# Host-laid parameters, memory and S5 array, S5's short kernels ahead of its scan, and gate blocks and branch work spread differently, in a one-core hybrid trunk

## The chip, the cores and the metric

One core of one Trainium2 chip runs the whole kernel. The metric is the device time of one execution in microseconds (us). TensorE is written PE, its weight loads PEld, VectorE DVE, ScalarE ACT, GpSimd POOL and SyncE SP; SP issues most of the DMA loads, POOL most of the stores.

## What is computed

One decoder layer on 1024 tokens of width 1024, all in float32, then a final norm:

```
h = rms_norm(x, norm_mix)
p_rw, p_s5, p_gla, p_gate = split(h @ w_in)
merged = sum_i sigmoid(p_gate_i) * (mixer_i @ w_branch_i)   # i: RWKV-7, S5, GLA
x += merged @ w_out
x += cross_attention(rms_norm(x), rms_norm(mem), ...)        # keys, values: mem_n @ xa_wkv
x += conv_ffn(rms_norm(x), ...)
```

S5 has 32 groups of 16 channels, each a complex diagonal recurrence of 64 states, `s_t = abar * s_(t-1) + B u_t`, `y = gelu(Re(C s) + d u)`, followed by `y * sigmoid(y @ w_glu + b_glu)`. RWKV-7 carries a 64 x 64 state for each of 8 heads through the 1024 tokens. The gates are 24 blocks of 128 columns of `w_in` (3 mixers x 8 blocks).

## The kernel before

A float32 product of full accuracy is three matmuls: both operands are split into a high and a low part in a rounded format (`split`, L145: ACT writes `whi`, DVE subtracts and writes `wlo`), and `mm3` (L161, the matmuls are L163 to L165) adds high x high, high x low and low x high. Weights come in units of 256 KB (`wunit`, L150: a DMA on SP's queue into `wraw`, then the split). `fm_block` (L172) makes 128 output columns for all 1024 tokens: 8 k-tiles x 2 halves x 3 = 48 matmuls of 512 columns into `ps_fm`. A gate block (`gate_block`, L1057) is one `fm_block`, a sigmoid on ACT and a store. Other matmuls (transposes, S5's and RWKV's products) are plain float32 with 128 columns.

The stages follow each other in program order. A scheduler orders each engine's instructions by priority, and a later, independent piece of work fills in where an earlier one waits; on each engine the order is then fixed.

- **start** (L258): the two memory tiles are loaded, transposed on PE, split into `mT`; the rows of small parameters (`vectors`, L86) come in by one DMA each and are turned to columns by a transpose on PE (`ps_v`). `kv_k` makes the keys (8 blocks of 24 matmuls of 256 columns; the eviction to `ko` multiplies by the memory's norm `mrb`), `x` is loaded, normed and transposed into `hT`, `kv_v` makes the values.
- **s5** (L357, `s5_states` L384): the parameters are loaded and transposed, powers of `abar` are computed on DVE. Then, for each of two halves of the groups: two `fm_block`s make `U` (via a DRAM array); per quad of groups `ps_ht` (transposes, copied by ACT to `ht`) and `ps_in` make the scan's input; DVE runs the scan (13 steps of 4 operations on `s5s`); ACT copies the states (L553, four copies); per quad a product on DVE makes `GA` (L558), PE the short kernel `ps_k` (L563), which goes to DRAM and comes back as `s5m` by eight loads (L573); ACT copies `GA` to `s5g` (L577); PE makes `ps_y` from both (L585, L586), ACT the gelu (L588), PE the transposes `ps_yt`. The `filler` of 11 gate blocks stands behind all this in the program. Then `s5h` is split and the GLU's 96 matmuls run.
- **gla**, then **rw_setup** and **rw1** with three gate blocks between its parts and ten behind it (`gates[14:]`).
- **rw2** (L909): 16 groups of four chunks. `rw2_prods` makes six products in a row, `vl`, `w1`, `x1`, `z`, `qm` among them, each copied out by ACT or DVE before it is an operand; `z` needs `w1`, `qm` needs `z`. `rw2_steps` carries the state: three matmuls for each chunk, then DVE and ACT each write half of the next state, on which the next chunk's third matmul waits. `fill` (in `run`) hands out the branch products of S5 and GLA in 16 pieces behind `step`.
- **conv_consts** (L122) loads and transposes the FFN's convolution weights late, before the attention.

Of the kernel before, what the change touches and what calls it, by code (L numbers as in the profile page):

```python
# [40 lines left out]
class Trunk:  # L41
# [44 lines left out]
    def vectors(self, p):  # L86


        nc, cp, A = self.nc, self.cp, self.A
        rows = [("nmem", A["norm_mem"], 8), ("nmix", A["norm_mix"], 8), ("mu", A["rw_mu"], 14), ("w0", A["rw_w0"], 4),  # L90
                ("a0", A["rw_a0"], 4), ("kk", A["rw_k_k"], 4), ("ka", A["rw_k_a"], 4), ("rk", A["rw_r_k"], 4),
                ("lnw", A["rw_ln_w"], 4), ("lnb", A["rw_ln_b"], 4), ("bglu", A["s5_b_glu"], 4),
                ("nxa", A["norm_xattn"], 8), ("nffn", A["norm_ffn"], 8), ("gkb", A["gla_gk_b"], 2), ("gnorm", A["gla_norm"], 1)]
        nrow = sum(n for _, _, n in rows)
        self.vc = cp.tile([128, nrow], F32, name="vc")
        self.cv = cp.tile([128, 176], F32, name="cv")
        self.omu = cp.tile([128, 14], F32, name="omu")
        self.omka = cp.tile([128, 4], F32, name="omka")
        self.vo = {}
        vr = [p.tile([n, 128], F32, name=f"vr{n}") for n in (16, nrow - 16)]  # L100

        def load(part, t, r0):
            for name, ap, n in part:
                o = self.vo[name] = sum(x[2] for x in rows[:[x[0] for x in rows].index(name)])
                flat = ap if len(ap.shape) == 1 else ap.rearrange("a b -> (a b)") if len(ap.shape) == 2 \
                    else ap.rearrange("a b c -> (a b c)")
                nc.sync.dma_start(t[o - r0:o - r0 + n, :], flat.rearrange("(n p) -> n p", p=128))

        def columns(t, r, n):
# [10 lines left out]
        load(rows[:2], vr[0], 0)  # L120
        columns(vr[0], 0, 16)
        return others  # L122

    def conv_consts(self):
        nc, A = self.nc, self.A
        with ExitStack() as c2:
            p = self.pool(c2, "crows")
            for i in range(2):
                r0, n = (0, 128) if i == 0 else (128, 48)
                vr = p.tile([128, 128], F32, name=f"cr{i}")  # L130
                if i == 0:
                    nc.sync.dma_start(vr[:, :], A["ffn_conv"].rearrange("a b c -> (a b c)").rearrange("(n p) -> n p", p=128)[0:128])
                else:
                    nc.sync.dma_start(vr[0:4, :], A["ffn_conv"].rearrange("a b c -> (a b c)").rearrange("(n p) -> n p", p=128)[128:132])
                    nc.sync.dma_start(vr[4:48, :], A["ffn_conv_b"].rearrange("a b -> (a b)").rearrange("(n p) -> n p", p=128))
                ps = self.psm.tile([128, 512], F32, tag="m", name="ps_cv")
                nc.tensor.transpose(ps[:, :n], vr[:n, :], self.ident[:n, :n])
                nc.vector.tensor_copy(self.cv[:, r0:r0 + n], ps[:, :n])
# [122 lines left out]
    def start(self, pool):  # L261

        self.hT = self.new_T(pool, "hT")
        with ExitStack() as c2:
# [17 lines left out]
            mem = [load(self.A["mem"][0, tt * 128:tt * 128 + 128, :]) for tt in range(2)]  # L282
            other_vectors = self.vectors(p)

            self.mT = {(k, l): p.tile([128, 256], F32R, name=f"mT{k}{l}") for k in range(8) for l in range(2)}
            self.to_fm(mem, "nmem", lambda k, l: self.mT[k, l][:])
            self.mrs = scales(mem)
            ones = p.tile([128, 128], F32, name="ones")
            self.nc.gpsimd.memset(ones[:], 1.0)
            self.mrb = p.tile([128, 256], F32, name="mrb")  # L290
            dg = p.tile([128, 256], F32, name="dg")
            for i in range(2):
                self.nc.vector.tensor_scalar(dg[:, i * 128:i * 128 + 128], self.ident[:], self.mrs[:, i:i + 1], None, op0=ALU.mult)
            ps = self.psm.tile([128, 512], F32, tag="m", name="ps_rb")
            self.nc.tensor.matmul(ps[:, :256], ones[:], dg[:], start=True, stop=True)
            self.nc.scalar.copy(self.mrb[:], ps[:, :256])
# [8 lines left out]
            self.kv_k(0)  # L305
            self.kv_k(1)
            load_x()
# [3 lines left out]
            norm_half(0)  # L311
            self.kv_v(0)
            norm_half(1)
            for j in range(1, 4):
                self.kv_v(j)
# [41 lines left out]
    def s5(self, filler):  # L357
# [4 lines left out]
        with ExitStack() as c1:  # L362
            po = self.pool(c1, "s5o")
            YT = [po.tile([128, T], F32, name=f"s5yt{b}") for b in range(4)]
            with ExitStack() as c2:
                p = self.pool(c2, "s5p")
                self.s5_states(p, YT, KD, UD)
                filler()
# [15 lines left out]
    def s5_states(self, p, YT, KD, UD):  # L384
# [3 lines left out]
        rows = p.tile([48, 128], F32, tag="kp", name="s5rows")  # L388
        ls = p.tile([48, 2], F32, name="s5ls")
        nc.sync.dma_start(rows[0:16, :], A["s5_a_re"][0].rearrange("(g r) n -> g (r n)", r=2))  # L390
        nc.sync.dma_start(rows[16:32, :], A["s5_a_im"][0].rearrange("(g r) n -> g (r n)", r=2))
        nc.sync.dma_start(ls[32:48, :], A["s5_log_step"][0].rearrange("(g r) -> g r", r=2))
        v.tensor_copy(rows[32:48, :].rearrange("p (r n) -> p r n", r=2), ls[32:48, :].unsqueeze(2).to_broadcast([16, 2, 64]))
        ps = self.psm.tile([128, 512], F32, tag="m", name="ps_s5")
        nc.tensor.transpose(ps[:, :48], rows[:, :], ident[:48, :48])
        par = p.tile([128, 48], F32, name="s5par")
        v.tensor_copy(par[:], ps[:, :48])
        ar, ai, lst = par[:, 0:16], par[:, 16:32], par[:, 32:48]
        B = [p.tile([128, 16, 16], F32, name=f"s5b{i}") for i in range(2)]
        C = [p.tile([128, 16, 16], F32, name=f"s5c{i}") for i in range(2)]  # L400
        for i, (bn, cn) in enumerate((("s5_b_re", "s5_c_re"), ("s5_b_im", "s5_c_im"))):
            nc.sync.dma_start(B[i][:], A[bn][0].rearrange("g n c -> (g n) c").rearrange("(g q) c -> q g c", q=128))
            cr = p.tile([128, 4, 64], F32, tag=f"hs{i}", name=f"s5cr{i}")
            nc.sync.dma_start(cr[:], A[cn][0].rearrange("g c n -> (g c) n").rearrange("(t q) n -> q t n", q=128))
            ps = self.psm.tile([128, 512], F32, tag="m", name="ps_c")
            for t in range(4):
                nc.tensor.transpose(ps[0:64, t * 128:t * 128 + 128], cr[:, t, :], ident[:])
            pv = ps[0:64, :].rearrange("p (g r c) -> p g r c", r=2, c=16)
            for r in range(2):
                v.tensor_copy(C[i][r * 64:r * 64 + 64], pv[:, :, r, :])  # L410
        dcol = p.tile([128, 4], F32, name="s5d")
        dr = p.tile([4, 128], F32, name="s5dr")
        nc.sync.dma_start(dr[:], A["s5_d"][0].rearrange("g c -> (g c)").rearrange("(t q) -> t q", q=128))
        ps = self.psm.tile([128, 512], F32, tag="m", name="ps_d")
        nc.tensor.transpose(ps[:, :4], dr[:], ident[:4, :4])
        v.tensor_copy(dcol[:], ps[:, :4])
# [70 lines left out]
        for hf in range(2):  # L487


            for b in range(2):  # L490
# [7 lines left out]
                for t in range(8):  # L498
                    nc.sync.dma_start(U[t * 16:t * 16 + 16, b * 8:b * 8 + 8, :], UD[c0:c0 + 128, t, :].rearrange("(g c) j -> c g j", c=16))
            for qd in range(2):  # L500
# [14 lines left out]
                for jj in range(2):  # L515
                    ps = self.psm.tile([128, 512], F32, tag="m", name="ps_in")
                    for j2 in range(2):
                        j = jj * 2 + j2
                        for i in range(2):
                            for r in range(2):  # L520
# [5 lines left out]
                                  ps[:].rearrange("p (g i j) -> p g i j", g=2, i=2))  # L526

# [381 lines left out]
    def rw2(self, p, p0, fill):  # L909
# [21 lines left out]
        n = 0  # L931
        todo, prev = [], []

        def step():
            pr, g, ops = todo.pop(0)
            with self.tc.high_priority(200):
                prev.append((pr, g, self.rw2_steps(p, pr, g, ops, S0)))
# [729 lines left out]
```

## Time and profile before

| | |
|---|---|
| median of 3 runs | 2225.42 us (2224.3 to 2226.51) |
| the profiled execution | 2228.63 us, its span 2226.9 us |
| mean granted PE clock | 0.988 |
| busy: PE, DVE, ACT, POOL | 2123.9, 1447.8, 961.0, 196.3 us |
| matmuls | 10,704 |

The span runs from the first to the last instruction on the profile; 1.7 us of the execution lie around it. PE's busy time is 95% of the span, so about 103 us of the span are its idle time. The clock of 1.00 is 2.4 GHz; the only other level is half of it. The busy shares are means over stages which differ; the rows below are from single stages.

### The profile page before, as it was taken

The page shows a single profiled execution, that of the slowest core. Times are in us where ns is not written, and L with a number is a line of the kernel's source. Part 1 is how long each engine was busy: PE and PEld are TensorE (multiplying, and loading weights), DVE is VectorE, ACT ScalarE, POOL GpSimd, SP SyncE. Part 2 cuts the span into 40 slices and gives each one's busy share as a digit, 9 for nine tenths or more (in the row PEclk, how much of TensorE's full clock was granted, in tenths as well). Part 3 has the DMA queues.
Part 4 walks back from the last instruction along what each step waited for, and adds up shares of the span by engine and source line. Part 5 has one row for each costly group of instructions (what it writes and reads, how often), then busy time and mean ns, then how long its engine had stood idle before and what let it go on. Part 6 is the DMA issues. An engine that isn't in the chain of part 4 may idle for free.

```text
span 2226.9 us, 29866 instructions
## 1 busy us (share of the span) xinstructions
PE 2123.9 (95%) x10704; PEld 1738.8 (78%) x10704; DVE 1447.8 (65%) x2870; ACT 961.0 (43%) x1667; POOL 196.3 (9%) x292
## 2 busy tenths in 40 slices
PE   7999989999999999999999999999899999988997
PEld 7878779888888888888788787877677777766886
DVE  7783733554667761667686656657777777777756
ACT  6324243553554431333343544446444444453452
POOL 1000000001211221002200000000011111110000
PEclk9999999999999999999999999999999999999999
DMA  7423331112334465665564232332565566588332
GB/s 246 137 88 95 94 97 54 29 52 67 134 112 128 135 186 152 171 157 141 136 214 148 87 104 72 89 119 81 137 157 159 139 150 128 123 241 286 104 96 102
DMA packets 318878, 286.65 MB, mean 129 GB/s; under 512 B 92532, under 2 KB 253129, under 8 KB 318729
## 3 DMA queue, kind: packets, MB, share of 16 engines
q1 hardware_dynamic: 291385, 207.64, 32.7%
q0 software_dynamic: 27344, 77.08, 12.7%
q8 instruction: 85, 1.39, 0.3%
q14 instruction: 64, 0.52, 0.1%
HBM read 190.32 MB, written 94.34 MB: 128 GB/s over the span
## 4 chain that ended last, share of the span: by engine, by line
PE 78%; DVE 10%; ACT 4%; DMA 4%; issue 2%; SPq 1%; DVEq 0%; ACTq 0%
PE ps_fm L163 10%; PE ps_fm L165 10%; PE ps_fm L164 10%; PE ps_q L1287 5%; PE ps_q L1288 5%; PE ps_q L1289 5%; PE ps_dm L1461 4%; PE ps_dn L1461 4%; PE ps_tm L163 3%; PE ps_tm L165 3%; PE ps_tm L164 3%; DVE wlo L148 2%; PE ps_g L868 1%; ACT whi L147 1%; DMA araw<-d_act 1%
## 5 line engine op out<-in xcount | busy, mean ns | idle before, releaser
L148 DVE TENSOR_TENSOR wlo<-wraw,whi 128x512 fp32r<-128x512 f32 (+1 forms) x318 | 219.7, 692 | 278.4 <-ACT whi L147 276.1
L147 ACT CAST whi<-wraw 128x512 fp32r<-128x512 f32 (+1 forms) x318 | 196.5, 619 | 472.0 <-PE ps_fm L164 283.0
L163 PE MATMUL ps_fm<-hT,whi 128*128 128x512 f32 x800 | 319.1, 399 | 0.0
L164 PE MATMUL ps_fm<-hT,whi 128*128 128x512 f32 x800 | 317.5, 397 | 0.0
L165 PE MATMUL ps_fm<-hT,wlo 128*128 128x512 f32 x800 | 317.4, 397 | 0.0
L163 PEld LDWEIGHTS ps_fm<-hT,whi 128*128 128x128 f32 x800 | 151.8, 190 | 33.1 <-issue 1.2
L165 PEld LDWEIGHTS ps_fm<-hT,wlo 128*128 128x128 f32 x800 | 151.5, 189 | 33.1 <-issue 0.6
L164 PEld LDWEIGHTS ps_fm<-hT,whi 128*128 128x128 f32 x800 | 151.8, 190 | 32.6 <-issue 0.8
L1287 PE MATMUL ps_q<-a,whi 128*128 128x512 f32 x336 | 134.9, 402 | 13.1 <-ACT u L1362 5.6
L1289 PE MATMUL ps_q<-a,wlo 128*128 128x512 f32 x336 | 134.1, 399 | 1.1 <-DVE wlo L148 1.1
L1288 PE MATMUL ps_q<-a,whi 128*128 128x512 f32 x336 | 134.0, 399 | 0.0
L1300 DVE SCALAR_TENSOR_TENSOR c<-u,cvn,c 128x1023 f32<-128x1023 f32 x84 | 107.7, 1283 | 22.2 <-ACT c L1298 20.8
L1309 POOL DMA_DIRECT2D d_act<-c x77 | 65.9, 862 | 438.5 <-DVE c L1304 320.5
L165 PE MATMUL ps_tm<-whi,a 128*128 128x512 f32 x256 | 101.3, 396 | 0.0
L1461 PE MATMUL ps_dn<-whi,b 128*128 128x512 f32 x312 | 98.6, 393 | 2.8 <-ACT whi L147 2.8
L147 ACT CAST whi<-s 128x512 fp32r<-128x512 f32 x84 | 52.1, 620 | 105.3 <-PE ps_q L1288 80.9
L147 ACT CAST b<-araw 128x512 fp32r<-128x512 f32 x72 | 44.7, 620 | 101.3 <-PE ps_dn L1461 37.6
L1287 PEld LDWEIGHTS ps_q<-a,whi 128*128 128x128 f32 x336 | 64.4, 192 | 29.5 <-ACT u L1362 6.9
L1461 PE MATMUL ps_dm<-whi,b 128*128 128x512 f32 x264 | 84.0, 398 | 2.4 <-ACT whi L147 2.4
L148 DVE TENSOR_TENSOR wlo<-s,whi 128x512 fp32r<-128x512 f32 x84 | 57.6, 688 | 36.3 <-ACT whi L147 35.3
L163 PE MATMUL ps_fm<-a,whi 128*128 128x512 f32 x192 | 78.7, 410 | 2.3 <-ACT whi L147 2.2
L148 DVE TENSOR_TENSOR b<-araw,b 128x512 fp32r<-128x512 f32 x72 | 49.6, 690 | 47.1 <-ACT b L147 46.9
(551 smaller groups left out, 5058.9 us busy)
## 6 DMA issues: line engine op xcount, KB each, us to landing
wraw<-in_w_in SPq DMA_DIRECT2D x104, 256.0 KB
araw<-d_act SPq DMA_DIRECT2D x77, 256.0 KB
d_act<-c POOLq DMA_DIRECT2D x22, 768.0 KB, 7.6
d_gate<-gate SPq DMA_DIRECT2D x24, 512.0 KB
gsg<-d_gate SPq DMA_DIRECT2D x24, 512.0 KB
wraw<-in_ffn_w_up SPq DMA_DIRECT2D x46, 256.0 KB
d_act<-c POOLq DMA_DIRECT2D x11, 1024.0 KB, 6.1
d_act<-c POOLq DMA_DIRECT2D x44, 256.0 KB, 5.1
```

The source lines that it names most:

```text
L147: self.nc.scalar.copy(hi, src)
L148: self.nc.vector.tensor_tensor(lo, src, hi.bitcast(F32), op=ALU.subtract)
L163: nc.tensor.matmul(ps, lh, rh, start=first, stop=False)
L164: nc.tensor.matmul(ps, lh, rl, start=False, stop=False)
L165: nc.tensor.matmul(ps, ll, rh, start=False, stop=last)
L868: nc.tensor.matmul(ps[:, j * 128:j * 128 + 128], BD[i][:, ci, :], AR[:, :, ci * 64:ci * 64 + 64], start=True, stop=True)
L1287: nc.tensor.matmul(ps, hi[:, s], t[0][:], start=first and k == 0, stop=False, skip_group_check=True)
L1288: nc.tensor.matmul(ps, hi[:, s], t[1][:], start=False, stop=False, skip_group_check=True)
L1289: nc.tensor.matmul(ps, lo[:, s], t[0][:], start=False, stop=last and k == 3, skip_group_check=True)
L1300: v.scalar_tensor_tensor(c[:, d:], src[:, :T - d], cw(2 - d), c[:, d:], op0=ALU.mult, op1=ALU.add)
L1309: to = lambda n0, n1, h, **kw: nc.gpsimd.dma_start(st(n0, n1), src[h].to_broadcast([128, n1 - n0, 512]), **kw)
L1461: nc.tensor.matmul(o, a[x][:, s], w[y], start=first and k == 0, stop=last and k == 2, skip_group_check=True)
```

## The change

The host lays out five things instead of the kernel: all small parameter columns (`cols`, one load to `vc`), the convolution columns (`conv`, one load to `cv`; `conv_consts` is gone), the S5 parameters as one array of 128 x 1076 values (`s5pk`, 551 KB, the first load on SP's queue), and the memory transposed (`memT`). The memory in its own layout is still loaded, for its norm, behind all of `x`; keys leave PE without the norm and are multiplied by `mrb` later, eight in a row.

```diff
+            for u in range(4):
+                self.nc.sync.dma_start(raw[u][:], self.A["memT"][u * 256:u * 256 + 256, :].rearrange("(k p) t -> p k t", p=128))
+                if u < 2:
+                    us.append(self.wunit(self.A["xa_wkv"][0][u * 512:u * 512 + 512, :128], 4, 128))
...
+            self.kv_k(0, us)
+            load_x()
+            self.kv_k(1)
+            self.kv_k(2)
+            self.kv_k(3)
+            load_x()
+            norm_half(0)
+
+            self.mrs = scales([load(self.A["mem"][0, tt * 128:tt * 128 + 128, :]) for tt in range(2)])
+            self.kv_v(0)
+            norm_half(1)
...
+            for j, o in enumerate(self.keys):
+                self.nc.vector.tensor_tensor(o[:], o[:], mrb[:], op=ALU.mult)
+                self.nc.gpsimd.dma_start(self.d_k[j * 128:j * 128 + 128, :], o[:])
```

In S5 the per-quad product `GA`, the short kernel `ps_k`, its way through DRAM and the loads of `s5m` (now two buffers) move ahead of the scan as `kernels(qd)`; the copies to `s5g` become `gains`, the first quad's ahead of the scan, the second's behind it. The gate blocks are handed out one place at a time: two behind `U`, three ahead of the scan, one behind it, for each half, and one before the GLU, 13 in all.

```diff
+            fill(2)
             for qd in range(2):
...
+            GA, M0 = kernels(0)
+            G0 = gains(GA)
+            GA, M1 = kernels(1)
+            fill(3)
...
                     nc.scalar.copy(S2[i * 64:i * 64 + 64, :, r, :], S[r * 64:r * 64 + 64, i, :, 0:128])
+            fill(1)
             for qd in range(2):
...
+                G, M = (gains(GA), M1) if qd else (G0, M0)
...
-                    self.gate_block(*gates[11 + pr])
+                    self.gate_block(*gates[13 + pr])
...
-            for g in gates[14:]:
+            for g in gates[16:]:
```

In rw2 the branch products are cut into 32 pieces (26 and 6, where there were 13 and 3) and handed out between `x1` and `z` and behind `qm`; the step of the group before stands between `z` and `qm`.

```diff
-                    todo.append((pr, hf * 2 + g2, self.rw2_prods(p, g2 * 4, t, R, c3)))
-                    if len(todo) > 1:
+                    z, qm = self.rw2_prods(p, g2 * 4, t, R, c3)
+                    fill()
+                    z()
+                    if todo:
                         step()
+                    todo.append((pr, hf * 2 + g2, qm()))
+                    norm()
+                    fill()
```

What the scheduler makes of it, at three places. First SP's queue at the program's beginning; `wraw<-in_xa_wkv` are the units of the key weights, two for each block of keys. Before:

```order
L269 DMA xt<-in_mem 128x1024 x2
L107 DMA vr_134<-in_norm_mem 8x128
L107 DMA vr_134<-in_norm_mix 8x128
L156 DMA wraw<-in_xa_wkv 128x4x128 x4
L269 DMA xt<-in_x 128x1024
L156 DMA wraw<-in_xa_wkv 128x4x128 x4
L269 DMA xt<-in_x 128x1024 x3
L156 DMA wraw<-in_xa_wkv 128x4x128
L269 DMA xt<-in_x 128x1024
```

And now:

```order
L1527 DMA s5pk<-in_s_par 128x1076
L95 DMA vc<-in_cols 128x81
L253 DMA memT_131<-in_memT 128x2x256
L122 DMA wraw<-in_xa_wkv 128x4x128
L253 DMA memT_132<-in_memT 128x2x256
L122 DMA wraw<-in_xa_wkv 128x4x128
L253 DMA memT_133<-in_memT 128x2x256
L253 DMA memT_134<-in_memT 128x2x256
L122 DMA wraw<-in_xa_wkv 128x4x128 x2
L235 DMA xt<-in_x 128x1024 x4
L122 DMA wraw<-in_xa_wkv 128x4x128 x4
L235 DMA xt<-in_x 128x1024
```

The memory's two tiles came first and the third key block's units stood behind one tile of `x`; now the S5 array, the columns and the first part of the memory come first, the memory's other parts among the first four units, and the third block's units stand behind four tiles of `x`.

Second, ACT's queue behind S5's first scan: `s5s` is the copy of the states (L553 before, L540 now), `s5g` the copy of `GA` (L577, L506), `s5yg` the gelu (L588, L553), `gate` the sigmoid of a gate block. Before:

```order
L553 COPY s5s_1652<-s5s 64x8x128 x4
L577 COPY s5g<-ga_1657 64x4x128 x2
L577 COPY s5g<-ga_1658 64x4x128 x2
L147 CAST whi<-wraw 128x512 x2
L1061 ACTIVATE gate<-ps_fm 128x1024
L147 CAST whi<-wraw 128x512 x2
L1061 ACTIVATE gate<-ps_fm 128x1024
L588 ACT_TABLE_LOAD
L588 ACTIVATE s5yg<-ps_y 128x4x8x16 x2
L577 COPY s5g<-ga_1718 64x4x128
```

And now, from the last sigmoid during the scan on:

```order
L1041 ACTIVATE gate<-ps_fm 128x1024
L540 COPY s5s_1985<-s5s 64x8x128 x4
L113 CAST whi<-wraw 128x512 x2
L1041 ACTIVATE gate<-ps_fm 128x1024
L113 CAST whi<-wraw 128x512
L553 ACT_TABLE_LOAD
L553 ACTIVATE s5yg<-ps_y 128x4x8x16 x2
L506 COPY s5g<-ga_1679 64x4x128
```

Of the first quad's copies to `s5g`, which stood between the copy of the states and the weight splits, nothing is left there; the second quad's still stand behind the first quad's gelu, which waits for PE.

Third, PE's queue in rw2 around one group. `ps_z` and `ps_qm` are the dependent products, `ps_p` with `s_` the state's matmul, `ps_fm` the branch work. Before:

```order
L979 MATMUL ps_w_8183<-R_8155,wx_7947 128x128 x4
L979 MATMUL ps_x_8190<-wv_7942,wak_7936 128x128 x4
L979 MATMUL ps_z<-qw_8188,qvl 128x128 x4
L163 MATMUL ps_fm<-a_7869,whi 128x512
L164 MATMUL ps_fm<-a_7870,whi 128x512
L165 MATMUL ps_fm<-a_7869,wlo 128x512
L163 MATMUL ps_fm<-a_7875,whi 128x512
L979 MATMUL ps_qm<-qz,wa_7939 128x128
L1013 MATMUL ps_p<-qx_8043,qz 128x128
L1014 MATMUL ps_p<-wv_7926,R_7969 128x128
L1016 MATMUL ps_p<-s_0_0_7952,qqm 128x128
```

And now:

```order
L951 MATMUL ps_z<-qw_8162,qvl 128x128
L993 MATMUL ps_p<-qx_8054,qz 128x128
L994 MATMUL ps_p<-wv_7863,R_7906 128x128
L996 MATMUL ps_p<-s_0_0_7889,qqm 128x128
L951 MATMUL ps_z<-qw_8162,qvl 128x128 x3
L129 MATMUL ps_fm<-a_7806,whi 128x512
L130 MATMUL ps_fm<-a_7807,whi 128x512
L131 MATMUL ps_fm<-a_7806,wlo 128x512
L993 MATMUL ps_p<-qx_8054,qz 128x128
L994 MATMUL ps_p<-wv_7863,R_7906 128x128
L996 MATMUL ps_p<-s_0_1_7891,qqm 128x128
L951 MATMUL ps_qm<-qz,wa_7876 128x128 x4
```

The three or four `ps_fm` matmuls between `ps_z` and `ps_qm` are still there, with a step of the chain among them; what is new is a run of 24 `ps_fm` matmuls right ahead of the first row, between `ps_x` and `ps_z`. In the whole of rw2 the runs of `ps_fm` number 77 before and 48 now.

## Rows read from the trace of the kernel before

**Rows 1.** the page's header, its engine row and its chain row.

```profile
span 2226.9 us, 29866 instructions
...
PE 2123.9 (95%) x10704; PEld 1738.8 (78%) x10704; DVE 1447.8 (65%) x2870; ACT 961.0 (43%) x1667; POOL 196.3 (9%) x292
...
PE 78%; DVE 10%; ACT 4%; DMA 4%; issue 2%; SPq 1%; DVEq 0%; ACTq 0%
```

**Rows 2.** windows: stretch, us, busy time and count per engine, PEclk, DMA share, GB/s.

```profile
0.00:20.00 20.00, 10.90 (x67) 10.01 (x67) 10.54 (x40) 12.28 (x23) 1.73 (x11) 1.00 0.89 274
20.00:40.00 20.00, 16.36 (x132) 15.71 (x131) 13.43 (x34) 12.86 (x25) 3.45 (x6) 1.00 0.83 267
74.13:330.22 256.09, 235.38 (x1213) 190.58 (x1212) 154.28 (x367) 85.10 (x121) 5.81 (x11) 0.96 0.33 97
884.33:1149.70 265.37, 252.84 (x1581) 213.80 (x1580) 192.12 (x460) 95.28 (x192) 28.20 (x30) 0.99 0.61 164
```

**Rows 3.** waits of PE in the S5 stage, 74 to 331 us: total, times, longest.

```profile
PE ps_k L563 <- DVE ga L332: 9.9, 2, 5.1
PE ps_ht L513 <- DVE hs L332: 2.6, 1, 2.6
PE ps_y L586 <- DMA s5m<-s_k: 2.5, 1, 2.5
PE ps_y L585 <- ACT s5g L577: 1.9, 1, 1.9
PE ps_fm L163 <- ACT s5h L147: 1.8, 1, 1.8
```

**Rows 4.** waits of PE in the start, 0 to 75 us.

```profile
PE ps_fm L163 <- DVE ko L1114: 2.6, 3, 1.8
```

**Rows 5.** PE's timeline: start, duration, engine, line, operation, [idle before].

```profile
74.13 0.48 PE L163 MATMUL ps_fm<-hT,whi 128*128 128x512 f32 x1
...
149.65 0.39 PE L164 MATMUL ps_fm<-hT,whi 128*128 128x512 f32 x1
...
158.84 0.39 PE L165 MATMUL ps_fm<-hT,wlo 128*128 128x512 f32 x1
164.29 0.40 PE L563 MATMUL ps_k<-ga,s5bd 128*32 128x128 f32 x2 [5.06 <-DVE ga L332]
```

**Rows 6.** DVE's timeline, S5's first scan: first operation, last, and the product's end.

```profile
129.52 1.23 DVE L538 TENSOR_TENSOR sc<-s5s,s5l 128x1024 f32<-128x1024 f32 x1
...
160.81 1.20 DVE L541 TENSOR_TENSOR s5s<-s5s,sc 128x1008 f32<-128x1008 f32 x1
...
166.43 0.46 DVE L559 TENSOR_SCALAR ga<-ga 128x576 f32<-128x576 f32 x1
```

**Rows 7.** ACT's timeline, behind S5's two scans.

```profile
162.05 4.21 ACT L553 COPY s5s<-s5s 64x1024 f32<-64x1024 f32 x4 [5.91 <-DVE s5s L541]
166.27 2.53 ACT L577 COPY s5g<-ga 64x512 f32<-64x512 f32 x4
...
288.96 1.28 ACT L588 ACT_TABLE_LOAD   x1
290.26 1.08 ACT L588 ACTIVATE s5yg<-ps_y 128x512 f32<-128x512 f32 x2
```

**Rows 8.** SP's queue in S5, 169 to 176 us.

```profile
169.81 0.34 SPq L570 DMA_DIRECT2D s_k<-kp  x1
...
172.37 3.82 SPq L573 DMA_DIRECT2D s5m<-s_k  x8
```

**Rows 9.** waits of PE in rw2, 884 to 1150 us.

```profile
PE ps_qm L979 <- DVE qz L997: 6.1, 6, 2.3
PE ps_fm L163 <- ACT whi L147: 2.2, 1, 2.2
```

**Rows 10.** PE's timeline in rw2: a 512-column group behind 128-column products.

```profile
994.42 0.50 PE L163 MATMUL ps_fm<-a,whi 128*128 128x512 f32 x1 [2.24 <-ACT whi L147]
994.76 0.39 PE L164 MATMUL ps_fm<-a,whi 128*128 128x512 f32 x1
```

More of the change, by code (lines that the diff above doesn't have):

```diff
@@ L382, in s5, with s5_states @@
                     nc.gpsimd.dma_start(self.ys5[j * 128:j * 128 + 128, :], sg[:])
-    def s5_states(self, p, YT, KD, UD):
+    def s5_states(self, p, pk, YT, KD, UD, fill):
         nc, A, v = self.nc, self.A, self.nc.vector
         ident = self.ident
[L388 to L416, printed above, removed]
@@ L417, in s5_states @@
+        ar, ai, lst, dcol = (pk[:, o:o + n] for o, n in ((0, 16), (16, 16), (32, 16), (48, 4)))
+        B, C = ([pk[:, o + i * 256:o + i * 256 + 256].rearrange("p (g c) -> p g c", g=16) for i in range(2)] for o in (52, 564))
         e16 = p.tile([128, 16], F32, name="e16")
@@ L526, in s5_states, with kernels, gains @@
                                   ps[:].rearrange("p (g i j) -> p g i j", g=2, i=2))
+            def kernels(qd):
+                g0 = hf * 8 + qd * 4
+                gs = slice(g0, g0 + 4)
+                GA = [p.tile([128, 4, 9, 16], F32, tag=f"hs{i}", name=f"ga{i}") for i in range(2)]
+                self.cmul(p, GA[0][:], GA[1][:], pb2(PW[0], gs), pb2(PW[1], gs), cb2(C[0], gs), cb2(C[1], gs), [4, 9, 16])
+                v.tensor_scalar(GA[1][:], GA[1][:], -1.0, None, op0=ALU.mult)
+                ps = self.psm.tile([128, 512], F32, tag="m", name="ps_k")
+                for j in range(4):
+                    for i in range(2):
+                        nc.tensor.matmul(ps[j * 32:j * 32 + 32, 0:128], BD[i][:, g0 + j].rearrange("p r c -> p (r c)"),
+                                         GA[i][:, j, 0:8, :].rearrange("p t c -> p (t c)"), start=(i == 0), stop=(i == 1))
+                kp = p.tile([128, 240], F32, tag="kp", name="kp")
+                v.memset(kp[:, 0:112], 0.0)
+                qg = hf * 2 + qd
+                v.scalar_tensor_tensor(kp[:, 112:128], e16[:], dcol[:, qg:qg + 1], ps[:, 0:16], op0=ALU.mult, op1=ALU.add)
+                v.tensor_copy(kp[:, 128:240], ps[:, 16:128])
+                nc.sync.dma_start(KD[qg * 8:qg * 8 + 8].rearrange("g c k -> (g c) k"), kp[:])
+                M = p.tile([128, 8, 128], F32, tag="m", name="s5m", bufs=2)
+                for t in range(8):
+                    nc.sync.dma_start(M[t * 16:t * 16 + 16], KD[qg * 8:qg * 8 + 8, :, t * 16:t * 16 + 128].rearrange("g c k -> c g k"))
+                return GA, M
+            def gains(GA):
+                G = p.tile([128, 4, 2, 128], F32, tag="ht", name="s5g")
+                for r in range(2):
+                    for i in range(2):
+                        nc.scalar.copy(G[i * 64:i * 64 + 64, :, r, :],
+                                       GA[i][r * 64:r * 64 + 64, :, 1:9, :].rearrange("p g t c -> p g (t c)"))
+                return G
+            GA, M0 = kernels(0)
+            G0 = gains(GA)
+            GA, M1 = kernels(1)
+            fill(3)
             X = S[:, :, :, 1:129]
@@ L1544, in run, with fill @@
         self.d_v = self.dr.tile([256, D], F32, name="d_v")
-        self.start(self.pool(left, "hT"))
-        self.s5(lambda: [self.gate_block(*g) for g in gates[:11]])
+        hT, c1 = self.pool(left, "hT"), ExitStack()
+        pk = self.pool(c1, "s5k").tile([128, 1076], F32, name="s5pk")
+        nc.sync.dma_start(pk[:], A["s5_par"])
+        self.start(hT)
+        todo = gates[:13]
+        def fill(n):
+            for _ in range(min(n, len(todo))):
+                self.gate_block(*todo.pop(0))
+        self.s5(c1, pk, fill)
         self.gla()
@@ L1610, in run @@
             self.query(hT, 0, j)
-        self.conv_consts()
         for j in range(0, 8, 2):
```

172 lines of the change are left out of this document (71 added, 101 removed).

## The prediction

> **What bounds the kernel now.** I read the page's engine row and its chain first. PE is busy for 95% of the span and holds 78% of the chain that ended last, DVE 10% [rows 1]: the bound is PE, and a change can gain only where PE waits, works at half its clock, or does work that goes away. The mean hides where that is, so the second view was the windows by stage [rows 2]. Three stages that the change touches stand out: the first 40 us, in which PE is idle for 9.1 and 3.6 us while the DMA engines are 0.89 and 0.83 busy; S5, 256.1 us with 20.7 us idle and a mean clock of 0.96; rw2, 265.4 us with 12.5 us idle and a clock of 0.99. Third, PE's waits in S5 [rows 3]: the largest are the two of 9.9 us together on `GA`, for which DVE has time only when the scan ends. The timeline shows it: PE has nothing from 159.2 on and starts `ps_k` at 164.29 [rows 5], while DVE ends its scan at 162.0 and the product at 166.9 [rows 6].
>
> The steady price of a 512-column matmul is read from two rows, 149.65 and 158.84 us, with 40 of them between [rows 5]: 0.2297 us, so a block of 48 is 11.0 us.
>
> **S5, the main term.** Before: 20.7 us idle, and a clock of 0.96 over 256.1 us, which is 0.04 x 256.1 = 10.2 us lost [rows 2]. Together 30.9 us. Two gate blocks more stand in the stage now, 22.1 us; two fewer behind rw1, where PE also works without a wait, so they cancel. What covers the later loads there is 22 us shorter; I cost that at nothing, because rw2's one wait behind a weight split is 2.2 us long [rows 9], and that is what it may grow by.
>
> After, by following the four queues in their new order with the durations of before, for each half:
> - The copies of `ps_ht` stand behind a gate's sigmoid on ACT. Before, PE waited once for 2.6 us at this place and not in the second half [rows 3]. I take 2.0.
> - `GA` and `ps_k` come ahead of the scan, with some 11 matmuls (2.5 us) between the pieces; no wait. The 9.9 us go.
> - From the last `ps_k` to the first `ps_y` PE has 143 matmuls, 32.9 us, against a scan of 32.5 us (129.52 to 162.01 [rows 6]) that starts a little earlier. Going through both orders from the last `ps_in` on, PE arrives 1.8 us behind the scan's end. But `ps_y` needs the four state copies, 4.2 us on ACT [rows 7]: PE waits for 2.5. This is what is late next.
> - The second quad's copies to `s5g`, 2.5 us, stand behind the first quad's gelu, 1.1 us for two [rows 7]; PE has 8 matmuls (1.8 us) there and waits for 1.7.
> - The last gelu ahead of `ps_yt`: 0.9.
>
> That is 7.1 us for each half, 14.2 together; a spell of half clock behind each pair of waits, 1.7 us, adds 3.4. So 17.6 us are lost where 30.9 were: 13.3 gained. The parameter transposes (`ps_s5`, `ps_c`, `ps_d`), the wait behind them and six fewer runs of matmuls add about 1.7. **S5 gains 15 us.** The bounds: 32 if nothing waits any more (30.9 + 1.7), 3 if the waits after the scan are twice what I count (14.2 + 3.4 more on 17.6).
>
> **The start.** The loads bound it, at 274 and 267 GB/s [rows 2]. Gained: the waits on `ko`, 2.6 us [rows 4], since keys are copied out to eight buffers; and, of the 12.7 us idle, what is not the first load, since the memory needs no transposes: the first block needs the S5 array, the columns, the whole memory and two units, 2.1 MB or 7.8 us at 274 GB/s, so about 4.5 us. Lost: the S5 array's 551 KB at the front of the queue are 2.0 us; four tiles of `x` (2.1 MB, 7.7 us) now stand ahead of the third block's units, and two blocks of 24 matmuls of half width are 5.6 us, so PE waits 2.1. The second memory load, 1.05 MB, is 3.9 us behind `x`; the last transposes of `hT` cover it, and if they didn't, all 3.9 would be lost. **Start: 3 us gained**, between 1 lost and 7 gained.
>
> What is first on the queue is paid in full by my sum. The Trainium skill, page "DMA: Bandwidth & Descriptors", section "Queues, rings and completion order", says that each DMA engine takes a queue's descriptors in ring order, which speaks against putting the S5 array first; by it the start pays the 2.0 us as counted, and if later units could pass it, the time would be 2 us less. The same page's table of measured bandwidth gives 425 GB/s for 16 MB; by that the start would gain some 3 us more, but the trace has 274, and the trace decides.
>
> **rw2.** A 512-column matmul takes 0.34 us to the next when the work before it was 128-column products (994.42 to 994.76 [rows 10]) against 0.23: 0.11 for each return. The order has 48 runs of branch matmuls instead of 77, so 29 x 0.11 = 3.2 us. The waits of `qm` on `z` are 6.1 us, six of them [rows 9]; following PE's order with 1.1 us between a `ps_z` and its `ps_qm` (an estimate: the four branch matmuls of 0.23 that stood between them before, and a little over) leaves two thirds of them, because a step of the chain now stands where branch work stood: 2.1 gained. **5 us**, between 5 lost (the chain's waits take the place) and 11.
>
> `conv_consts` and the small loads: two transposes, two copies, sixteen loads less, mostly beside other work: 1 us, between 0 and 2.
>
> **The sum**: 3 + 15 + 5 + 1 = 24 us. The profiled execution took 2228.63 us (1.7 of it outside the span), so it would take 2204.6; it was 3.2 above the median, and the forecast for the median is 2225.4 - 24 = **2201 us**.
>
> **Rivals.**
> - *The waits go altogether* (14%). DVE's scan may run faster without its companions, and PE then never waits at `ps_y`: S5 gains up to 32, rw2 11, the start 4: 2178. For it: only two waits in S5 have no matmul to stand in for them. Against it: the copies of 4.2 us are still on ACT behind the scan. Half of it gives 2190.
> - *The waits move behind the scan* (17%). State copies, sigmoid, gelu and second-quad copies are one chain on ACT; if the sigmoid or a split ahead of the gelu waits for PE, which waits for them, each half loses 7 us more, S5 gains about 3, the start nothing: 2225.4 - 3 - 5 - 1 = 2216. For it: 4.4 us of just such waits in the second half of before, `s5m` and `s5g` [rows 3].
> - *SP's queue holds back the weights* (9%), and the kernel gets slower. From `s_k`'s store to the last `s5m` load SP is taken for 6.4 us (169.81 to 176.19 [rows 8]), and now ahead of the scan, where PE lives on weight units. If fewer than two units (24 matmuls, 5.5 us each) are split ahead there, PE loses 6.4 us and half a clock spell of 1.7 in each of four quads: 32 us, against 24 gained: 2233. Against it: the DMA engines are 0.33 busy in S5 [rows 2], and units were ahead at all times but the scan's end.
> - *It does not do what it says* (5%): PE's order has a step between `z` and `qm`, not branch work, and the gate blocks only change places. Then S5 pays later what it saves, and the time stays within 2221 to 2230.
>
> **How the numbers follow.** The forecast's own case, 2192 to 2210, gets 55%. About 0.2%, 4.5 us, is what a measurement can tell from no change. Faster by more: 55 + 14 + 17 = 86%; within: 5%; slower: 9%. The range takes the forecast's case, the upper half of the first rival and nearly all of the second: 2184 to 2219; outside it lie about 4% below and 16% above.
>
> **What would show it.** `ps_k` should vanish from PE's waits in S5; `ps_y` should wait on the copy of the states for 2 to 3 us in each half and on `s5g` for under 2; the S5 stage, with its two blocks more, should be 263 us at a clock of 0.99. The first `ps_fm` on `hT`, at 74.13 before [rows 5], should start near 71. In rw2 the waits of `qm` should be near 4 us. The prediction is wrong if `ps_fm` waits on `whi` or `wlo` ahead of the scan (the third rival), if PE's idle time in S5 stays above 20 us, or if the first `hT` matmul starts later than 75.

## The result and the profile after

The changed kernel takes **2210.32 us** (median of 4 runs, 2208.99 to 2216.17) where the kernel before, run beside it, takes 2225.97 (4 runs, 2224.3 to 2229.76): a ratio of 0.9936 [0.9921, 0.995]. Faster, as forecast, by 15.65 us between the medians where 24 were forecast (the ratio, which is taken over all the runs, makes it 14); 2201 was forecast, and the range of 2184 to 2219 holds the time. A second set of runs of the same kernel (e6 below) gave 0.9943 [0.9928, 0.9958].

The page's header, engine row and chain row of the changed kernel, to be laid beside [rows 1]:

```profile
span 2214.4 us, 29751 instructions
...
PE 2121.2 (96%) x10674; PEld 1739.2 (79%) x10674; DVE 1451.0 (66%) x2863; ACT 957.2 (43%) x1669; POOL 196.1 (9%) x292
...
PE 79%; DVE 9%; ACT 5%; DMA 4%; issue 2%; SPq 0%; DVEq 0%; ACTq 0%
```

PE still is the bound. Its share of the span is a point higher; its idle time, span less busy time, fell from 103.0 to 93.2 us. The windows of the changed kernel, the first two over the stretches of [rows 2], the third S5 from its first matmul to the first of GLA, the fourth from the first matmul of rw2 to the first of the FFN (in us: length; busy time and count of PE, PEld, DVE, ACT, POOL; clock; DMA share; GB/s):

```profile
0.00:20.00 20.00, 9.39 (x48) 8.37 (x48) 8.09 (x27) 11.56 (x23) 1.73 (x11) 1.00 0.98 303
20.00:40.00 20.00, 18.95 (x144) 18.74 (x145) 12.90 (x30) 8.95 (x18) 0.00 (x0) 0.91 0.86 285
75.10:329.84 254.74, 251.12 (x1298) 203.16 (x1297) 156.90 (x363) 86.06 (x124) 7.61 (x15) 0.99 0.36 107
861.88:1547.71 685.83, 656.34 (x3465) 539.93 (x3463) 455.54 (x1000) 290.22 (x598) 33.46 (x40) 0.99 0.45 126
```

The same five stages, cut at the same matmuls in three executions (us; in brackets PE's idle time):

| stage | before | after | after, again (e6) |
|---|---|---|---|
| start, to the first matmul on `hT` | 74.1 (14.8) | 75.1 (15.3) | 74.4 (14.5) |
| S5, to the first of GLA | 256.1 (20.7) | 254.7 (3.6) | 254.7 (3.6) |
| GLA to the end of rw1's gate blocks | 554.1 (6.2) | 532.0 (6.2) | 532.1 (6.2) |
| rw2, branches, attention, to the FFN | 675.9 (21.7) | 685.8 (29.5) | 681.6 (29.8) |
| FFN and norm | 666.7 (39.6) | 666.7 (38.7) | 663.2 (36.4) |

S5 does 22.05 us more work (two gate blocks of 48 matmuls, 0.2297 us each [rows 5]) in 1.4 us less, so it gained 23.4 us; the third stage is shorter by just those two blocks. The start lost 1 us (0.2 in e6), and the stage of rw2 lost 9.9 in the one execution and 5.7 in the other. The two executions of one kernel differ by 8 us, nearly all of it behind rw1: stage times there are good to some 4 us, while the three stages ahead differ by 0.7 at most.

Where S5's time came from is in PE's waits in the changed kernel's S5 (total, times, longest), beside [rows 3]:

```profile
PE ps_y L550 <- ACT s5s L540: 2.5, 2, 1.2
PE ps_y L550 <- ACT s5g L506: 0.9, 1, 0.9
```

`ps_k` and `ps_ht` are gone. What is left is behind the scan. DVE's timeline has the end of the first scan at 170.97 (169.76 and 1.21), ACT's the copies of the states, PE's what it did meanwhile (start, duration, then [idle before]):

```profile
169.76 1.21 DVE L528 TENSOR_TENSOR s5s<-s5s,sc 128x1008 f32<-128x1008 f32 x1
```

```profile
171.00 4.23 ACT L540 COPY s5s<-s5s 64x1024 f32<-64x1024 f32 x4 [7.89 <-DVE s5s L528]
```

```profile
172.64 0.40 PE L131 MATMUL ps_fm<-hT,wlo 128*128 128x512 f32 x1
173.16 0.49 PE L550 MATMUL ps_y<-s5g,s5s 128*128 128x128 f32 x2
173.59 0.46 PE L551 MATMUL ps_y<-s5m,s5u 128*128 128x128 f32 x2
175.28 0.52 PE L550 MATMUL ps_y<-s5g,s5s 128*128 128x128 f32 x2 [1.24 <-ACT s5s L540]
```

PE's last matmul of the gate block starts at 172.64, so with the steady 0.23 us the next could start at 172.87, 1.9 us behind the scan's end (I had 1.8). PE then does not wait for all four copies: the first group of `ps_y`, four matmuls of which two take the states, starts at 173.16, when two copies are done. The wait, 1.24, is for the rest.

### The profile page after: what moved, and what is told of

Read it like the earlier page. It is cut to its first block, busy times and chain, and to the rows that moved or that the text cites. A ratio compares the mean times of both kernels' runs of the same rounds, so it can differ in the third digit from the quotient of the medians.

```text
span 2214.4 us, 29751 instructions
## 1 busy us (share of the span) xinstructions
PE 2121.2 (96%) x10674; PEld 1739.2 (79%) x10674; DVE 1451.0 (66%) x2863; ACT 957.2 (43%) x1669; POOL 196.1 (9%) x292
## 4 chain that ended last, share of the span: by engine, by line
PE 79%; DVE 9%; ACT 5%; DMA 4%; issue 2%; SPq 0%; DVEq 0%; ACTq 0%
PE ps_fm L129 11%; PE ps_fm L131 11%; PE ps_fm L130 10%; PE ps_q L1267 5%; PE ps_q L1268 5%; PE ps_q L1269 5%; PE ps_dm L1441 4%; PE ps_dn L1441 4%; PE ps_tm L129 3%; PE ps_tm L131 3%; PE ps_tm L130 3%; DMA araw<-d_act 1%; ACT whi L113 1%; PE ps_g L833 1%; DVE wlo L114 1%
## 5 line engine op out<-in xcount | busy, mean ns | idle before, releaser
L1267 PEld LDWEIGHTS ps_q<-a,whi 128*128 128x128 f32 x336 | 64.7, 193 | 29.5 <-ACT u L1342 6.7
```

The source lines that it names most:

```text
L1267: nc.tensor.matmul(ps, hi[:, s], t[0][:], start=first and k == 0, stop=False, skip_group_check=True)
```

## The experiments

All are edits of the changed kernel, and each ratio is to the kernel before on the same chip.

**e1: rw2 in its old order.** The product's two halves joined again, `fill` behind the step, 16 pieces.

```diff
-                    z, qm = self.rw2_prods(p, g2 * 4, t, R, c3)
-                    fill()
-                    z()
-                    if todo:
-                        step()
-                    todo.append((pr, hf * 2 + g2, qm()))
-                    norm()
-                    fill()
+                    todo.append((pr, hf * 2 + g2, self.rw2_prods(p, g2 * 4, t, R, c3)))
+                    if len(todo) > 1:
+                        step()
```

> The changed kernel with rw2 as it was before (six products in a row, branch work in 13 and 3 pieces behind the step). My reading of the two profiles: from rw2's first product to the first FFN matmul the change lost 10 us (675.9 before, 685.8 now), because ps_z now waits for DVE, where the copy of w1 stands behind the norm's small operations (8.8 us), and the state's chain waits (6.3 us). If so, this kernel is 7 to 11 us faster than the changed one: 2199 to 2203. Rival: the loss in rw2 belongs to that one profiled execution (it took 2216, the others 2209 to 2211); then it is within 3 us of 2210.

2213.22 us, 0.995 [0.9937, 0.9962]. The theory that the new order costs 10 us fell: the stage takes 685.7 us with the old order and 685.8 with the new. The rival fell too, by which the loss belongs to the one execution. PE's waits in rw2, the changed kernel first, then e1:

```profile
PE ps_p L993 <- ACT s L1000: 6.3, 10, 1.0
PE ps_z L951 <- DVE rs_b L192: 4.6, 2, 3.0
PE ps_z L951 <- DVE rs_y L193: 2.2, 2, 1.9
PE ps_z L951 <- DVE rs_b L191: 2.0, 1, 2.0
PE ps_qm L951 <- DVE qz L973: 1.8, 1, 1.8
```

```profile
PE ps_qm L944 <- DVE qz L962: 10.0, 6, 3.4
PE ps_z L944 <- DVE qw L955: 5.7, 5, 3.5
```

Old and new order of the products differ in which product waits: `qm` 10.0 us with the old one, 1.8 with the new, where `z` and the state's `ps_p` wait instead. PE's idle time in the stage is about the same, 28.4 and 29.5 us.

**e2: the start's queue.** The S5 array's load goes behind the memory's second load, the first load of `x` behind the second key block.

```diff
             self.kv_k(0, us)
-            load_x()
             self.kv_k(1)
+            load_x()
...
+            self.nc.sync.dma_start(pk[:], self.A["s5_par"])
             self.kv_v(0)
...
-        nc.sync.dma_start(pk[:], A["s5_par"])
```

> The changed kernel with two loads moved on SP's queue: the S5 array behind all of x and the memory, and the first four x tiles behind the second pair of key blocks, as before. Theory: the start gains nothing in the changed kernel because PE waits 8.75 us for its first matmul with the S5 array ahead, and 2.5 us, with a half-clock spell behind it, for the third key block's units behind x. If so, PE starts near 6.9, the wait near 18 us is gone, S5 starts at 69 to 72 instead of 75.1, and the time is 3 to 6 us less: 2204 to 2207. Rival: the start is bound by the sum of the loads, which is 1.6 MB more than before, and by the values behind the memory's second load; then S5 still starts at 74 to 76 and the time is 2209 to 2211.

2205.87 us, 0.9918 [0.9904, 0.9933], as the theory had it; the interval overlaps that of the changed kernel, so the stage has to show it. PE's timeline in the changed kernel:

```profile
8.75 0.58 PE L129 MATMUL ps_fm<-mT,whi 128*128 128x256 f32 x1 [8.75 <-ACT whi L113]
...
20.65 0.39 PE L129 MATMUL ps_fm<-mT,whi 128*128 128x256 f32 x1 [2.47 <-ACT whi L113]
```

and in e2, with its first two windows:

```profile
6.69 0.58 PE L129 MATMUL ps_fm<-mT,whi 128*128 128x256 f32 x1 [6.69 <-ACT whi L113]
```

```profile
18.27 0.39 PE L129 MATMUL ps_fm<-mT,whi 128*128 128x256 f32 x1 [1.27 <-ACT ko L1095]
```

```profile
0.00:20.00 20.00, 11.89 (x62) 10.88 (x63) 10.85 (x31) 11.56 (x22) 1.73 (x11) 1.00 0.89 269
20.00:40.00 20.00, 19.74 (x161) 18.63 (x159) 13.57 (x32) 11.63 (x22) 0.00 (x0) 1.00 0.94 309
```

The first matmul starts 2.06 us earlier, which is the S5 array's place on the queue (2.0 in my sum). The third key block starts at 18.27 instead of 20.65; its wait of 2.47 us for the weights is gone, and one of 1.27 for the copies out of the keys (`ko`) stands there. The window from 20 to 40 us, whose clock was 0.91 behind the wait of 2.47, has 1.00. The stage ends at 71.45.

**e3: the short kernels behind the scan again**, the gate blocks where the change puts them; and **e4: the kernels ahead, but no gate block placed**: all 13 stand in the program behind both halves.

```diff
-            GA, M0 = kernels(0)
-            G0 = gains(GA)
-            GA, M1 = kernels(1)
             fill(3)
...
-                G, M = (gains(GA), M1) if qd else (G0, M0)
+                GA, M = kernels(qd)
+                G = gains(GA)
```

```diff
-            fill(2)
...
-            fill(3)
...
-            fill(1)
```

> The changed kernel with the short kernels (GA, ps_k, the loads of s5m, the copies to s5g) behind the scan again, the gate blocks left where they are. Theory: the S5 stage gained its 23 us (two blocks more in a shorter stage) because nothing DVE makes stands between the scan and ps_y; then the waits of PE on GA come back, about 5 us in each half, and those on s5m and s5g, with half-clock spells: 14 to 22 us slower than the changed one, 2224 to 2232. Rival: placing the gate blocks is what helps, and the short kernels' place hardly matters: within 5 us, 2210 to 2215.

> The changed kernel with all 13 gate blocks behind the two halves in the program, as the 11 were before, the short kernels ahead of the scan. Theory: the scheduler pulls blocks forward wherever PE would wait, as it did before, so the explicit places are worth little: within 4 us of the changed kernel, 2207 to 2214. Rival: the places carry the gain; then S5 loses 8 us or more, 2218 and up.

e3: 2212.58 us, 0.9946 [0.9934, 0.9958]. e4: 2223.95 us, 1.0 [0.9991, 1.0009]. In both the rival was right. The window of S5 in e3, then in e4, and PE's waits in e4's S5:

```profile
74.60:332.61 258.01, 249.26 (x1298) 203.89 (x1297) 156.92 (x363) 86.75 (x125) 7.58 (x15) 0.99 0.36 105
```

```profile
74.09:340.13 266.04, 251.65 (x1298) 206.21 (x1297) 156.46 (x363) 89.23 (x126) 7.62 (x15) 0.97 0.34 102
```

```profile
PE ps_y L547 <- ACT s5s L538: 9.0, 2, 4.6
PE ps_ht L465 <- DVE hs L311: 5.3, 1, 5.3
```

Against 278.1 us (256.1 and the two blocks), the stage gains 20.1 with placed gate blocks and late kernels, 12.1 with early kernels and no block placed, 23.4 with both. Each of the three contains what the host's S5 array saves (ten transposes and a wait of 1.4 us for the parameters); no run shows that share by itself, nor S5 with neither of the two moves. Each move covers much of what the other does: the early kernels take the 9.9 us on `GA` away, but without matmuls laid by for the scan's end PE then waits 9.0 us for the states there. With the blocks placed, kernels behind the scan still find work beside them: in e3 PE waits for `GA` for 1.2 us. The order that I had taken for the main term is worth 3.3 us once the blocks are in place.

**e5: 11 gate blocks in S5**, 10 behind rw1, as before the change.

```diff
-        todo = gates[:13]
+        todo = gates[:11]
...
-                    self.gate_block(*gates[13 + pr])
+                    self.gate_block(*gates[11 + pr])
...
-            for g in gates[16:]:
+            for g in gates[14:]:
```

> The changed kernel with 11 gate blocks in S5 instead of 13, so that 10 and not 8 stand behind rw1, as before. The kernel with the old rw2 code lost the same 10 us in rw2 as the changed one, so the loss is not from the new order of the products. Theory: it comes from the stage in front, two gate blocks (22 us) shorter, which shifts what the scheduler knows to be ready when rw2 begins; then rw2 to the first FFN matmul takes 676 to 680 us again and the time, with S5 losing nothing, is 2200 to 2204. Rival: the number of blocks has nothing to do with it: the stage stays at 684 to 687 and S5 loses some of its cover, 2208 to 2216.

2218.28 us, 0.9982 [0.997, 0.9994], above what theory and rival forecast. Windows of S5 and of rw2 to the FFN, and PE's waits in S5:

```profile
74.45:322.05 247.60, 231.37 (x1203) 187.16 (x1201) 154.17 (x359) 82.07 (x119) 7.61 (x15) 0.97 0.34 101
876.18:1551.09 674.91, 649.97 (x3465) 534.30 (x3463) 453.26 (x1000) 289.96 (x598) 33.98 (x40) 1.00 0.43 127
```

```profile
PE ps_y L550 <- ACT s5s L540: 12.2, 2, 11.0
```

Half of the theory held: with ten blocks behind rw1 the stage of rw2 is at 674.9 us, where it was before, although it has the new order. But S5, with 22.05 us less to do, is only 7.1 us shorter: 15 lost. One of the last two of the 13 blocks is what PE does at the end of the second scan: from the last `ps_k` to `ps_y` it has 95 `ps_fm` matmuls instead of 143, and `ps_y` waits there for 11.0 us. Smaller waits, and a clock of 0.97 instead of 0.99, are the rest. So blocks that I costed as "two more here, two fewer there, they cancel" are worth 15 us in S5 and cost 7 to 11 behind rw1.

**e6: the changed kernel again** on e5's chip, no edit.

> The changed kernel unaltered, beside the others on the same chip. Every theory: ratio to before 0.9925 to 0.995, 2208 to 2212 us where before takes 2225.

2210.7 us, 0.9943 [0.9928, 0.9958]; its stages are in the table above.

**e7: `w1` copied by ACT instead of DVE**, past the norm's small operations in DVE's queue.

```diff
-            v.tensor_copy(w1[:], ps)
+            nc.scalar.copy(w1[:], ps)
```

> The changed kernel with w1 copied out of PSUM by ACT instead of DVE, so that the copy no longer stands behind the norm's operations on DVE. Theory: PE's waits of ps_z on DVE (about 10 us with qw and the rs_ operations) fall below 3 us, and the time is 6 to 9 us less: 2201 to 2204. Rival: ACT has vl, x1 and the state's second half to write in the same place, the wait changes its name only: within 3 us of the changed kernel.

2208.51 us, 0.9933 [0.9917, 0.9949]: not to be told from the changed kernel, as the rival had it. PE's waits on the norm's operations are gone in rw2, and those of `ps_p` on ACT went from 6.3 to 10.7 us: for the larger part a new name for the same wait.

**e8: e2 with 15 gate blocks in S5** (one more ahead of each scan) and six behind rw1.

```diff
-            fill(3)
+            fill(4)
...
-        todo = gates[:13]
+        todo = gates[:15]
```

> The kernel of the two moved loads (2205.9 where before took 2223.7) with four gate blocks instead of three ahead of each scan, 15 in all. Theory: the last waits of S5, 1.2 us on the state copies and 0.9 on s5g in each half, vanish, since PE comes 11 us later to ps_y: S5 gains 2 to 4 us, 2202 to 2204. Rival: the two blocks fewer behind rw1 make rw2 lose more than that (13 instead of 11 cost it 10 us): 2206 or more.

2208.81 us, 0.993 [0.9916, 0.9943]; the rival. S5's window and PE's largest wait from 800 us on:

```profile
72.21:343.05 270.84, 270.21 (x1394) 219.36 (x1393) 160.79 (x371) 90.47 (x130) 9.16 (x18) 1.00 0.37 109
```

```profile
PE ps_vl L952 <- DMA wa<-rw_tm: 13.3, 1, 13.3
```

S5 is now without a gap, 0.6 us idle in 270.8 us. What it gained is lost again in front of rw2: the loads of `rw_tm`, RWKV's operands, aren't there when the six blocks are done, and PE stands for 13.3 us. With six blocks, this is the cover behind rw1 that I costed at nothing; with the eight of the changed kernel PE doesn't wait there.

**e9: most of the norm's small operations on POOL** (ten of twelve), out of DVE's queue; **e11: the same with e2**.

```diff
-        rs = self.rsqrt_small(p, m[:, 1], 1 / 64, 64e-5, 2, 8, 64)
+        rs = self.rsqrt_pool(p, m[:, 1], 1 / 64, 64e-5, 2, 8, 64)
```

> The changed kernel with ten of the twelve small operations of rw2_norm's reciprocal root on POOL instead of DVE (the two with integer shifts stay). Theory: rw2 loses because these operations, some 0.19 us each and up to 1.2 us where a POOL add runs beside them, stand ahead of the copies of w1 and z on DVE; with them gone PE's waits of ps_z and ps_qm on DVE, 12 us in the changed kernel, fall below 5 and the kernel is 5 to 9 us faster, ratio 0.990 to 0.992. Rival: the chain is latency, not occupation, and moves with it; POOL's adds and the chain now hold each other up, or the waits move to ps_p on the state (6.4 us now): within 3 us of the changed kernel, 0.993 to 0.9955.

> The two moved loads of the start (ratio 0.9918 alone) and the reciprocal root on POOL together. If both act and do not touch each other: ratio 0.987 to 0.990, 2194 to 2201 where before takes 2223. If POOL gives nothing: 0.991 to 0.9925, 2203 to 2207.

e9: 2232.94 us, 1.0045 [1.0029, 1.0061]; e11: 2230.65 us, 1.0035 [1.0022, 1.0047]. Both slower than the kernel before, and worse than either theory. DVE's largest wait in e9's rw2 (861 to 1160 us), and PE's:

```profile
DVE ysb L1035 <- POOL rs_y L208: 35.1, 15, 3.5
```

```profile
PE ps_z L966 <- DVE qw L977: 12.8, 6, 4.6
PE ps_p L1008 <- ACT s L1015: 9.6, 11, 3.0
PE ps_yt L1038 <- DVE ysb L1035: 5.6, 3, 2.2
```

DVE executes in its fixed order: the operation that uses the norm, `ysb`, now waits for POOL 15 times, 35.1 us in all, and `w1`'s copy (into `qw`) stands behind it. A shorter queue was exchanged for a wait in the same queue.

**e10: 13 gate blocks in S5, one between rw1's parts, ten behind it**; **e12: the same with e2**.

```diff
-                if pr < 3:
+                if pr < 1:
                     self.gate_block(*gates[13 + pr])
...
-            for g in gates[16:]:
+            for g in gates[14:]:
```

> The changed kernel with 13 gate blocks in S5, one instead of three between rw1's parts, and ten instead of eight behind rw1. Theory: rw2's stage depends on how much work stands right ahead of it; with ten it took 675 to 676 us, with eight 682 to 686; then it is back at 674 to 678, and if rw1 does not miss the two blocks the kernel is 5 to 9 us faster, ratio 0.990 to 0.992. Rival: rw1 needs them (its parts wait for DVE, 10 us or more in idle time come back), or the number ahead has nothing to do with it: ratio 0.994 or more.

> The two moved loads of the start (ratio 0.9918 alone) and the 13, 1 and 10 gate blocks (0.9932 alone, where the changed kernel has 0.9936 and 0.9943) together. If the two gains add up: 0.990 to 0.992, 2199 to 2204 where before takes 2222, rw2's stage at 675 to 678 us and S5 starting near 71. If the order in rw2 comes out otherwise because the start is shorter: 0.992 to 0.9935, the stage at 680 or more.

e10: 2207.53 us, 0.9932 [0.9916, 0.9947]; e12: 2202.85 us, 0.9919 [0.9906, 0.9931]. The stage of rw2 was as the theory had it, e12's ratio too; e10's ratio lies between theory and rival. The window of rw2 to the FFN in e10, and PE's waits in its rw2:

```profile
864.63:1541.53 676.90, 651.33 (x3465) 535.47 (x3463) 453.43 (x1000) 290.26 (x598) 33.96 (x40) 0.99 0.43 126
```

```profile
PE ps_p L993 <- ACT s L1000: 4.8, 7, 1.7
PE ps_fm L131 <- DVE wlo L114: 2.9, 1, 2.9
PE ps_z L951 <- DVE rs_b L192: 1.8, 2, 1.6
```

With ten blocks ahead of it the stage is back at 676.9 us while S5 keeps its 13; but GLA to rw1, which has two blocks fewer between its parts, takes 535.7 us instead of 532.0 to 532.1. Net 1 to 5 us by stages, and by ratios not to be told from the changed kernel. e12 has the lowest time of all, and its interval overlaps those of the changed kernel ([0.9921, 0.995] and [0.9928, 0.9958]) only at their lower ends; by ratio it equals e2, so that the move of the two gate blocks adds to e2 isn't shown.

## Why the prediction was right, and where it was wrong

*The direction and the place were right.* PE was the bound, its idle time in S5 the thing to gain, and 23.4 us came from there. None of the rivals took place as a whole; in S5 alone the first, in which the waits go altogether, came nearest. `ps_fm` waits on no split ahead of the scan, so SP's queue holds back nothing (the third rival); what is left behind the scan is 3.4 us for both halves, so the chain on ACT didn't grow (the second).

*S5: 15 forecast, 23.4 measured.* "14.2 together" for the new waits was the mis-sized term: PE's whole idle time in the stage is 3.6 us. By its parts: `ps_ht`, 2.0 in each half, didn't appear; `ps_y` on the states, 2.5 in each, measured 2.5 for both, because four matmuls need two copies only; `s5g`, 1.7 in each, 0.9 for both; the last gelu none. From waits and clock 25.6 us should have come (30.9 less 3.6 and 1.7, half of the 3.4 us that PE worked at 1.2 GHz), so the 1.7 that I added for transposes and switches isn't seen. The lower bound of 3 was a wrong sum: twice the 17.6 are 35.2 us, more than the 30.9 and 1.7 that could be gained, so 2.6 lost; the "about 3" of the second rival is likewise 1 (15 less twice 7). The stage's 263 us at a clock of 0.99 were 254.7 at 0.99. The reason was also only half of it: "`GA` and `ps_k` come ahead of the scan ... the 9.9 us go" is true of the waits, but by e3 and e4 the gate blocks' places give 20.1 us and the kernels' 12.1, overlapping and with the host's array in both; early kernels without the blocks move a good part of the wait.

*The start: 3 gained forecast, 1 lost.* The first matmul on `hT` starts at 75.10, past the 75 that I had named as the sign of a wrong step (in e6 at 74.36). Both losses were there: 2.06 us for the S5 array (2.0), and, where 2.1 was counted for the tiles of `x`, waits of 2.47 and 0.41 us with 3.4 us at half clock behind them, 4.6 in all. The gains of 2.6 and 4.5 were together too high. Four kernels have e2's start, which takes both losses away; they end the stage at 71.45 (e2), 72.21 (e8), 68.85 (e11) and 69.48 (e12), which is 1.9 to 5.3 gained on before's 74.13 and not 7.1. They spread with what DMA moved in their first 20 us: 269, 246, 280 and 280 GB/s.

The Trainium skill, page "DMA: Bandwidth & Descriptors", section "Queues, rings and completion order", states that each DMA engine takes a queue's descriptors in ring order. e2's 2.06 us agrees with that.

*rw2: 5 gained forecast; by e1, none.* The waits of `qm` fell further than I said, 6.1 to 1.8 us (near 4), and `z` and `ps_p` took over. That is what I had named as the lower bound, "the chain's waits take the place". e1 shows that it isn't the new order's doing: the old order waits as long at this point. With ten blocks ahead of rw2 the new order takes 674.9, 676.9 and 677.4 us (e5, e10, e12) and the old 675.9 (before): within what executions differ by. The 3.2 us for fewer returns can't be found either. Their price was misread: the row at 994.42 stands behind a wait of 2.24 us [rows 10], and in the 65 returns of before's rw2 without a wait the median to the next matmul is 0.315 us, which makes it 2.5.

*"So they cancel", and a shorter cover "at nothing": the step that failed.* It hides the loss of 6 to 10 us. The gate blocks right ahead of rw2 number ten before the change, in e5, in e10 and in e12: the stage takes 674.9 to 677.4 us. With eight (the changed kernel, e1 to e4, e6) it takes 681.6 to 685.8, and 679.4 in e7. With six it takes 676.4, with 13.3 us of waiting ahead of it (e8). I looked for one wait that would grow, on a weight split. What grew is `ps_z` on the operations of the norm's reciprocal root (`rs_b`, `rs_y`): 8.8 us with eight blocks, in the changed kernel and in e6, 1.8 in e10; against it stands a wait of 2.9 us on a split in e10. PE's idle time in the stage, 29.8 us in e6 and 25.6 in e10, is 4.2 of the 4.7 us between these two; in the first execution more half-clock stretches behind such waits come on top. PE's order in rw2 is one and the same in the changed kernel, e2, e3, e4 and e6, and another in e5, e10 and e12, where 118 of its 1644 matmuls stand elsewhere. So the number of blocks ahead and the scheduler's order in rw2 changed together. Why two blocks less should cost time when PE doesn't stop in front of rw2 is left open: which of the two does it, and which row of the order, wasn't tried.

*`conv_consts` and the rest, 1 us*: not tried alone. From the last `ps_yt` of rw2 to the FFN the time falls from 400.2 to 396.8 us, but with 17 matmuls fewer, and 15 more stand in rw2; nothing is left to see.

So 24 became 15.65: S5 gave 8 more than forecast, the start 4 less, and the stage of rw2 11 to 15 less than its 5. That the total came out as near as it did is in part luck: errors of opposite sign made up for each other.

## What to carry to other kernels

Work that fills waits isn't free to move: ask what it covered where it stood, by name, and what arrives there late (with six blocks, RWKV's operands), before costing it at nothing. Filling work that is placed at the wait can be worth more than shortening the chain that causes the wait, and the two overlap, so try each alone. In an in-order queue, moving a chain's operations to another engine can exchange the queue's length for a wait of the whole queue behind the result, as e9 and e11 did.

## What the runs showed of the hardware

A tiny operation can be slow because of its neighbour. The norm's operations of 64x8 take 0.16 us on DVE. In the changed kernel seven of the 192 in rw2 took 0.86 to 1.23 us, here two of them. DVE's timeline, then POOL's and PE's at that time:

```profile
1030.41 0.16 DVE L189 TENSOR_SCALAR rs_y<-rs_i 64x8 int32<-64x8 int32 x1
...
1031.81 0.87 DVE L191 TENSOR_TENSOR rs_b<-rs_y 64x8 f32<-64x8 f32 x1
1032.71 1.19 DVE L192 SCALAR_TENSOR_TENSOR rs_b<-rs_x,rs_b 64x8 f32<-64x8 f32 x1
1033.93 0.16 DVE L193 SCALAR_TENSOR_TENSOR rs_y<-rs_b,rs_y 64x8 f32<-64x8 f32 x1
1034.01 0.68 DVE L962 COPY qw<-ps_w 128x512 f32<-128x512 f32 x1
```

```profile
1031.39 2.48 POOL L1072 TENSOR_TENSOR a<-a,gsg 128x512 f32<-128x512 f32 x2 [5.03 <-DVE gsg L1071]
```

```profile
1034.84 0.46 PE L951 MATMUL ps_z<-qw,qvl 128*128 128x128 f32 x2 [1.96 <-DVE rs_b L191]
```

The two additions on POOL are of 1.24 us each, so they end at 1032.63 and 1033.87; the two operations on DVE end at 1032.68 and 1033.90. Each ended within 0.05 us of the addition that it ran into. PE's next `ps_z`, whose operand `qw` DVE copies right behind them, waited 1.96 us, put down to one of them.

The Trainium skill, page "SBUF — State Buffer", section "Who interferes with whom", states that an operation of DVE with two inputs in SBUF contends with one of GpSimd that reads SBUF, over a shared port pair that is an exclusive lock, and that issue order decides which of the two is held up. These rows agree: the operations at 1031.81 and 1032.71 have two inputs (the first takes `rs_y` twice), and each began after one of POOL's additions had begun.

The second is the spread between executions of one kernel: with the same matmuls, rw2 to the FFN took 685.83 us in the first execution of the changed kernel, with PE busy for 656.34, and in e6, by its window:

```profile
861.20:1542.80 681.60, 651.83 (x3466) 536.00 (x3464) 454.64 (x1000) 289.95 (x598) 33.81 (x40) 0.99 0.44 127
```

Idle times are alike (29.5 and 29.8), so the difference lies in PE's busy time: by the granted clock PE is at 1.2 GHz for 17.1 us in the first and for 6.8 in the second. A change worth 5 us in such a stage can't be read from one profile.
